# Seven block products for eight in the second product of the second block's MLP

## The chip, the cores and the metric

The kernel runs on one core of a Trainium2 chip. The metric is the device time of one execution in microseconds (us). Names of the engines: PE is TensorE (matrix products), DVE is VectorE, ACT is ScalarE, POOL is GpSimd, SP is the engine that issues most DMAs. SBUF and PSUM are the on-chip memories: products arrive in PSUM, in banks of 128 partitions by 512 fp32 values.

## The reference, cut to what matters

Two transformer blocks follow each other on 512 tokens of width 1024, all in fp32. The change lies in the last stage, the MLP of the second block, whose hidden width is 4096:

```python
def _sq_relu_mlp(h, w1, w2):
    return jnp.square(jax.nn.relu(h @ w1)) @ w2
```

Its result goes through an RMS norm with a gain and is added to the residual stream x, which is the output. `h @ w1` is the first product ("up"), the one with `w2` the second product ("down").

## The kernel before

**Precision.** Every fp32 operand is split into a high and a low part that the one-pass matrix format holds: `split` writes the high part on ACT (L147) and the low part, source less high part, on DVE (L148; for a few weights on POOL). `mm3` (L152 to L154) makes one product out of three matmuls, high by high, high by low, low by high. Weights are split chunk by chunk: a chunk of 128 by 1024 values is fetched by a DMA that SP issues into a raw buffer (two of them), and `parts` takes a buffer for either part out of a ring of PARTS = 5. A chunk can be split only when the one five places ahead of it has been used by PE.

**The MLP** (`mlp`, L822, called at the end of `dense_two`) takes the hidden width in four groups of 1024, that is 8 chunks j of 128. In a group first comes "up": for each j 24 matmuls of 512 columns (8 chunks of the contraction by 3) into a bank `m2up`, then relu on ACT (L843, tile `m2re`), its square on DVE (L844, `m2sq`), and the split of the square (`m2hid`), 512 columns wide. The first five chunks of all run in two token halves, each with 24 matmuls of 256 columns, while the last tokens of h are still being prepared. Then comes "down": hidden activations are the stationary operand, weights `m2d` the moving one. For each of two halves of the output columns, 4 weight chunks by 4 token tiles by 2 by 3 matmuls, 96 in all, each of 512 columns; so 192 to a group. The partial sums (`evac2`) are copied on ACT in group 0 (L1278) and added on DVE to `y` in the other groups (L1280). In the last group every finished half goes on: squares on ACT (L1243), two or three tiny instructions on POOL (L1245 to L1248) for 1 / rms, the gain on DVE (L1288), and x += y / rms on DVE (`post`, L1255), then the output's DMA.

**Around it.** `evac1` closes the output projection ahead of it token tile by token tile: x is fetched, y's squares and 1 / rms (ACT, POOL), x += y / rms (L1255, DVE), x's squares and 1 / rms, then `mod_T` transposes the tile on PE and splits it into `h2T`. x stays in SBUF until the end. The banks of PSUM are dealt out in rings: three for the second product, three for "up".

A scheduler sets the order in which each engine's instructions stand in the program; each engine then works through its own queue in that order.

## Time and profile before

| | us |
|---|---|
| three timed executions | 1271.0, 1275.27, 1275.59 |
| their median | 1275.27 |
| the profiled execution: span from first to last instruction | 1270.8 |

The profile gives no time of its own for the profiled execution beside the span. Its page lists busy time of each engine, the chain of work that ended last, and groups of instructions. A busy PE in it means that matmuls were in flight; how fast they follow each other is read from their starts. The granted clock is the share of full speed that TensorE was granted.

### The profile page before, as it was taken

Reading aid. Unit: us, or ns where it says so; the run is one execution under the profiler, and the core shown is the slowest. Engines: PE = TensorE matmul, PEld = TensorE weight load, DVE = VectorE, ACT = ScalarE, POOL = GpSimd, SP = SyncE. Lnnn points to the kernel's source line nnn. Section 1 sums busy time; section 2 is a strip of 40 time slices with the busy share of each in tenths; the row PEclk is TensorE's granted clock in tenths of the full one; section 3 lists DMA queues with packets and bytes.
Section 4 is the critical chain, followed back from the end, with each engine's and each line's share of the span. In section 5 each row is a group of like instructions: output and inputs, shape, how many; then the busy total and the mean of one; then the engine's idle time right before and its main releaser. Section 6 shows DMA issues by size and latency. Waiting matters only on the chain. (4 is left out here: it accounts for less than half of the span.)

```text
span 1270.8 us, 16908 instructions
## 1 busy us (share of the span) xinstructions
PE 1227.1 (97%) x6388; PEld 1027.8 (81%) x6388; DVE 750.8 (59%) x1320; ACT 539.2 (42%) x1032; POOL 257.5 (20%) x328
## 2 busy tenths in 40 slices
PE   7889999999999999999999999999999999999997
PEld 7889887779888788888888777778888888888886
DVE  4799666597897854336364567564752343433534
ACT  6677555434223324235263556454652331422431
POOL 3877551261020000000023114212400000000001
PEclk9899999999999999999999999999999999999999
DMA  5232121464678733143254122215232322412412
GB/s 163 64 73 68 26 63 67 133 186 148 198 239 257 234 100 116 63 131 122 67 176 129 51 67 74 64 59 178 82 117 83 100 100 67 130 69 67 149 50 84
DMA packets 147290, 140.22 MB, mean 110 GB/s; under 512 B 14025, under 2 KB 115160, under 8 KB 147208
## 3 DMA queue, kind: packets, MB, share of 16 engines
q1 hardware_dynamic: 143384, 131.02, 33.4%
q0 software_dynamic: 3824, 8.12, 2.1%
q8 instruction: 50, 0.82, 0.3%
q14 instruction: 32, 0.26, 0.1%
HBM read 134.85 MB, written 4.26 MB: 109 GB/s over the span
## 5 line engine op out<-in xcount | busy, mean ns | idle before, releaser
L898 DVE SCALAR_TENSOR_TENSOR macc<-mod,silu_c,macc 128x1024 f32<-128x1024 f32 x56 | 76.7, 1379 | 13.8 <-DMA mod<-in_w_mod_dram 13.7
L1245 POOL TENSOR_SCALAR ss<-ss 128x1 f32<-128x1 f32 x4 | 1.8, 442 | 328.5 <-ACT sk L1243 328.5
L1280 DVE TENSOR_TENSOR y<-m2d,y 128x512 f32<-128x512 f32 x24 | 16.6, 691 | 60.4 <-PE m2d L154 60.3
L975 DVE SCALAR_TENSOR_TENSOR xa<-m1d,r,xa 128x512 f32<-128x512 f32 x32 | 23.8, 745 | 37.2 <-PE m1d L154 37.2
L147 ACT ACTIVATE m2hid<-m2sq 128x512 fp32r<-128x512 f32 x32 | 20.2, 631 | 38.9 <-DVE m2sq L844 38.9
L147 ACT ACTIVATE m1hid<-m1sq 128x512 fp32r<-128x512 f32 x32 | 20.0, 629 | 38.1 <-DVE m1sq L844 38.1
L918 POOL DMA_DIRECT2D modrows<-mrow x8 | 3.9, 492 | 147.3 <-DVE mrow L916 92.8
L148 DVE TENSOR_TENSOR m2hid<-m2sq,m2hid 128x512 fp32r<-128x512 f32 x32 | 22.1, 691 | 19.0 <-ACT m2hid L147 18.9
L148 DVE TENSOR_TENSOR npl<-t,nph 128x512 fp32r<-128x512 f32 x32 | 21.7, 681 | 16.4 <-ACT nph L147 16.3
L181 POOL TENSOR_SCALAR w<-w,g_attn 128x384 f32<-128x384 f32 x20 | 26.1, 1314 | 11.2 <-DMA w<-in_w_in_dram 6.6
L148 DVE TENSOR_TENSOR m1hid<-m1sq,m1hid 128x512 fp32r<-128x512 f32 x32 | 21.9, 686 | 9.1 <-ACT m1hid L147 9.1
L194 POOL TENSOR_SCALAR p<-p,d 128x512 f32<-128x512 f32 x8 | 14.0, 1752 | 56.6 <-DVE d L1116 26.3
L683 DVE TENSOR_REDUCE mb<-sb 128x1 f32<-128x128 f32 (+3 forms) x32 | 15.6, 486 | 16.7 <-PE sb L680 16.6
L1115 ACT ACTIVATE p<-s,m 128x512 f32<-128x512 f32 x32 | 22.0, 688 | 6.2 <-DVE m L1113 6.2
L685 ACT ACTIVATE pb<-sb,mb 128x128 f32<-128x128 f32 (+3 forms) x32 | 16.8, 525 | 16.4 <-DVE mb L683 16.1
L843 ACT ACTIVATE m1re<-m1up 128x512 f32<-128x512 f32 x32 | 18.6, 582 | 9.0 <-PE m1up L154 8.7
L1069 POOL TENSOR_TENSOR tb<-G,nam 128x256 f32<-128x256 f32 x24 | 17.7, 765 | 22.6 <-DVE m L1109 12.5
L147 ACT ACTIVATE nph<-t 128x512 fp32r<-128x512 f32 x32 | 19.0, 595 | 7.4 <-PE t L1126 7.2
L844 DVE SCALAR_TENSOR_TENSOR m1sq<-m1up,m1re 128x512 f32<-128x512 f32 x32 | 21.8, 681 | 0.1
L844 DVE SCALAR_TENSOR_TENSOR m2sq<-m2up,m2re 128x512 f32<-128x512 f32 x32 | 21.8, 682 | 0.0
L1126 PE MATMUL t<-ident,p 128*128 128x128 f32 x128 | 18.4, 276 | 1.9 <-DVE npl L148 1.9
L147 ACT ACTIVATE pbh<-tb 128x128 fp32r<-128x128 f32 (+3 forms) x32 | 13.8, 434 | 14.9 <-PE tb L703 14.7
(1856 smaller groups left out, 4521.8 us busy)
## 6 DMA issues: line engine op xcount, KB each, us to landing
mod<-in_w_mod_dram SPq DMA_DIRECT2D x48, 512.0 KB, 4.5
m1u<-in_w_up_dram SPq DMA_DIRECT2D x32, 512.0 KB, 4.5
m1d<-in_w_down_dram SPq DMA_DIRECT2D x32, 512.0 KB, 3.6
m2u<-in_w_mlp_in_dram SPq DMA_DIRECT2D x32, 512.0 KB, 4.2
m2d<-in_w_mlp_out_dram SPq DMA_DIRECT2D x32, 512.0 KB, 3.4
w<-in_w_in_dram SPq DMA_DIRECT2D x16, 512.0 KB, 4.2
w<-in_w_in_dram SPq DMA_DIRECT2D x48, 128.0 KB, 2.6
o1w<-in_w_out_dram SPq DMA_DIRECT2D x8, 512.0 KB, 3.6
```

Of the source, the lines that this page charges most:

```text
L147: self.nc.scalar.activation(out=hi, in_=src, func=AF.Copy)
L148: (eng or self.nc.vector).tensor_tensor(out=lo, in0=src, in1=hi.bitcast(F32), op=ALU.subtract)
L181: eng.tensor_scalar(out=rv[:, i], in0=rv[:, i], scalar1=g, scalar2=None, op0=ALU.mult)
L685: ac(out=pr[:, 0:n], in_=s[:, 0:n], func=AF.Exp, bias=m[:, 0:1], accum_out=den[:, 0:1])
L843: ac(out=r, in_=acc, func=AF.Relu)
L844: nc.vector.scalar_tensor_tensor(out=s, in0=acc, scalar=0.0, in1=r, op0=ALU.max, op1=ALU.mult)
L898: nc.vector.scalar_tensor_tensor(out=accs[s], in0=rw, scalar=sc[:, s, k:k + 1], in1=accs[s], op0=ALU.mult, op1=ALU.add)
L975: nc.vector.scalar_tensor_tensor(out=x[t][:, cols], in0=acc, scalar=r2[:, t:t + 1], in1=x[t][:, cols], op0=ALU.mult, op1=ALU.add)
L1069: nc.gpsimd.tensor_tensor(out=tb[:, h, y], in0=G[:, h, ::-1, o:o + 32][:, :, ::-1], in1=nam[:, y, :].unsqueeze(1).to_broadcast([P, 8, 32]) ...
L1115: ac(out=pr, in_=s, func=AF.Exp, bias=m[:, 2:3], accum_out=den[:, 0:1])
L1126: nc.tensor.transpose(out=tps[:, j * P:(j + 1) * P], in_=pr[:, j * P:(j + 1) * P], identity=self.ident)
L1280: nc.vector.tensor_tensor(out=y[t][:, cols], in0=acc, in1=y[t][:, cols], op=ALU.add)
```

## The change

"Down" of the first three groups is done in Strassen's manner (Winograd's form). The group's 1024 hidden columns, 512 tokens and 1024 output columns are each cut in two: even and odd chunks j, tokens 0 to 255 and 256 to 511, columns 0 to 511 and 512 to 1023. Eight products of quarter blocks would give the group's sum; seven are made instead, out of sums and differences of blocks:

- `operands` forms, for every pair of chunks j, four sums of the pair's squares on DVE (L1301 to L1304 of the changed kernel, 128 by 256 values each), and splits them together (128 by 1024). The even chunk's first half is split alone (256), the odd chunk whole (512).
- `block` fetches quarter blocks of the weights; two of the six needed are fetched a second time, so 12 DMAs of 512 KB to a group instead of 8. `less` subtracts blocks on POOL (L1365), eight instructions of 128 by 1024 to a group.
- `times` makes one product: two chunks of weights, two token tiles, 24 matmuls of 512 columns. The order is 1, 5, 6, 2, 4, 3, 7. Each product has its own accumulator of 256 tokens by 512 columns (`Y`), kept over the groups, filled by ACT in group 0 (L1355) and added to by DVE afterwards (L1357): 14 instructions of 128 by 512 to a group instead of 8.
- `join` combines the seven accumulators on POOL into the four quarters of the output, 14 additions of 128 by 512, while the last group's "up" runs. The last group is done plainly, as before, and added to them.
- SBUF is dealt out anew for this: x is written to DRAM in `evac1` (a DMA that POOL issues) and fetched again for the end, and "down" has five banks of PSUM instead of three.

```diff
@@ Build.run @@
+            self.xspill2 = self.dp.tile([SEQ, D], F32, name="xspill2")
...
@@ dense_two @@
-        self.row(gg[:, 1, :], 5)
-        x = [self.xp.tile([P, D], F32, tag=f"x{t}", name=f"xb{t}") for t in range(NT)]
+            x = [self.ep.tile([P, D], F32, tag=f"x{t}", name=f"xb{t}", bufs=1) for t in range(NT)]
...
+                    nc.gpsimd.dma_start(out=self.xspill2[t * P:(t + 1) * P, :], in_=x[t])
+                    self.mod_T(x[t], g, hT, t, f"n4_{t}", rx)
+            self.out_proj_rows(a["w_out_2"][0], self.mixT, evac1, "o2", KPS2)
+        self.banks(a=(0, 1, 2, 3, 4), s=S2)
+        with ExitStack() as ph:
+            self.ep = ph.enter_context(tc.tile_pool(name="ep3", bufs=2, reuse_waits="tile"))
+            self.mlp_seven(hT, a["w_mlp_in_2"][0], a["w_mlp_out_2"][0], y, gg, "m2")
+
+    def mlp_seven(self, hT, w1, w2, y, gg, name):
+        tt = nc.vector.tensor_tensor
+        pt = nc.gpsimd.tensor_tensor
+        G = 8
+        NG = NJ // G
+        quads = [self.quad(f"{name}hid{i}").rearrange("p a b c -> p (a b c)") for i in range(2)]
+        hid = quads + [ep.tile([P, 3584], F32R, tag=f"hid{i}", name=f"{name}hid{i + 2}", bufs=1) for i in range(2)]
+        more = ep.tile([P, 4, 512], F32, tag="more", name=name + "more", bufs=1)
+        Y = {q: [y[i][:, h * 512:h * 512 + 512] for h in range(2)] for i, q in enumerate((2, 3, 4, 6))}
+        Y[1] = [more[:, 0], more[:, 1]]
+        Y[5] = [more[:, 2], more[:, 3]]
+        Y[7] = [gg[:, 1, h * 512:h * 512 + 512] for h in range(2)]
+        sums = gg[:, 0, :].rearrange("p (o t) -> p o t", o=4)
+        def operands(g, p, st):
+            a11, a21, a12, a22 = st[:, 0, 0:256], st[:, 0, 256:512], st[:, 1, 0:256], st[:, 1, 256:512]
+            tt(out=sums[:, 0], in0=a21, in1=a22, op=ALU.add)
+            tt(out=sums[:, 2], in0=a11, in1=a21, op=ALU.subtract)
+            tt(out=sums[:, 1], in0=sums[:, 0], in1=a11, op=ALU.subtract)
+            tt(out=sums[:, 3], in0=a12, in1=sums[:, 1], op=ALU.subtract)
+            hi, lo = parts_of(p)
+            self.split(hi[:, 3:7], lo[:, 3:7], sums)
+            self.split(hi[:, 1:3].rearrange("p o t -> p (o t)"), lo[:, 1:3].rearrange("p o t -> p (o t)"), st[:, 1])
+        def parts_of(p):
+            return [hid[p][:, x * 1792:(x + 1) * 1792].rearrange("p (o t) -> p o t", o=7) for x in range(2)]
+        def plain(j):
+            return hid[j % G // 2][:, j % 2 * 1024:j % 2 * 1024 + 1024].rearrange("p (x t) -> p x t", x=2)
+        def up(j, st):
+            wh, wl = self.weights(f"{name}u{j}", [(0, self.kview(w1, 0, KC, j * P, P))], KC, P, eng=nc.gpsimd if j < WPJ else None)
+            acc = self.ps("s", f"{name}up{j}")
+            nsp = 2 if j < NSP else 1
+            w = SEQ // nsp
+            for sp in range(nsp):
+                cols = slice(sp * w, (sp + 1) * w)
+                for k in range(KC):
+                    hqd = hT[k // 4]
+                    self.mm3(acc[:, cols], wh[:, k, :], wl[:, k, :], hqd[:, k % 4, 0, cols], hqd[:, k % 4, 1, cols], k == 0, k == KC - 1)
+            s = st[:, j % 2]
+            ac(out=s, in_=acc, func=AF.Relu)
+            nc.vector.scalar_tensor_tensor(out=s, in0=acc, scalar=0.0, in1=s, op0=ALU.max, op1=ALU.mult)
+            if j // G == NG - 1:
+                self.split(plain(j)[:, 0], plain(j)[:, 1], s)
+            elif j % 2 == 0:
+                hi, lo = parts_of(j % G // 2)
+                self.split(hi[:, 0], lo[:, 0], s[:, 0:256])
+        def block(g, q, r, c):
+            t = ep.tile([P, 1024], F32, tag="rb", name=f"{name}d{g}{q}{r}{c}", bufs=6).rearrange("p (a b) -> p a b", a=2)
+            j = g * G + 4 * q
+            src = w2[j * P:(j + 4) * P, c * 512:c * 512 + 512].rearrange("(i r p) e -> r p i e", r=2, p=P)[r]
+            nc.sync.dma_start(out=t, in_=src)
+            return t
+        def times(g, n, o, b):
+            accs = [self.ps("a", f"{name}p{g}{n}{tau}") for tau in range(2)]
+            for q in range(2):
+                wh, wl = self.parts(f"{name}w{g}{n}{q}", b[q], 2, 512)
+                for tau in range(2):
+                    rows = slice(tau * P, (tau + 1) * P)
+                    for i in range(2):
+                        hi, lo = parts_of(2 * q + i)
+                        self.mm3(accs[tau], hi[:, o, rows], lo[:, o, rows], wh[:, i, :], wl[:, i, :], q == i == 0, q == i == 1)
+            for tau in range(2):
+                if g == 0:
+                    ac(out=Y[n][tau], in_=accs[tau], func=AF.Copy)
+                else:
+                    tt(out=Y[n][tau], in0=accs[tau], in1=Y[n][tau], op=ALU.add)
+        def down(g):
+            def blocks(r, c):
+                return [block(g, q, r, c) for q in range(2)]
+            def less(out, b, c):
+                for o, x, z in zip(out, b, c):
+                    pt(out=o, in0=x, in1=z, op=ALU.subtract)
+            b11 = blocks(0, 0)
+            times(g, 1, 0, b11)
+            t1 = blocks(0, 1)
+            less(t1, t1, b11)
+            times(g, 5, 3, t1)
+            t2 = blocks(1, 1)
+            less(t2, t2, t1)
+            times(g, 6, 4, t2)
+            b21 = blocks(1, 0)
+            times(g, 2, 1, b21)
+            less(b21, t2, b21)
+            times(g, 4, 2, b21)
+            b22 = blocks(1, 1)
+            times(g, 3, 6, b22)
+            b12 = blocks(0, 1)
+            less(b22, b22, b12)
+            times(g, 7, 5, b22)
+        def join():
+            for out, p, q, op in ((2, 1, 2, ALU.add), (1, 1, 6, ALU.add), (7, 1, 7, ALU.add), (6, 7, 5, ALU.add), (4, 7, 4, ALU.subtract),
+                                  (5, 1, 5, ALU.add), (3, 5, 3, ALU.add)):
+                for tau in range(2):
+                    pt(out=Y[out][tau], in0=Y[p][tau], in1=Y[q][tau], op=op)
+        s_banks = self.rings["s"]
+        self.rings["s"] = s_banks + list(MORE)
+        for g in range(NG):
+            for j in range(g * G, (g + 1) * G):
+                if j == NSP:
+                    self.rings["s"] = s_banks
+                if j % 2 == 0:
+                    st = ep.tile([P, 2, SEQ], F32, tag="st", name=f"{name}sq{j // 2}", bufs=2)
+                up(j, st)
+                if j % 2 == 1 and g < NG - 1:
+                    operands(g, j % G // 2, st)
+            if g < NG - 1:
+                down(g)
+        join()
+        self.row(gg[:, 1, :], 5)
+        x = []
+        for t in range(NT):
+            x.append(ep.tile([P, 1024], F32, tag="rb", name=f"xc{t}", bufs=6))
+            nc.sync.dma_start(out=x[t], in_=self.xspill2[t * P:(t + 1) * P, :])
+        ss2 = [self.small("ss", f"ss2{t}") for t in range(NT)]
+        for half in range(2):
+            def evac(t, acc):
+                z = Y[((2, 3), (4, 6))[t // 2][half]][t % 2]
+                tt(out=z, in0=acc, in1=z, op=ALU.add)
+                r = self.squares(z, ss2[t], half, f"sk{half}{t}", "st")
+                tt(out=z, in0=z, in1=gg[:, 1, half * 512:half * 512 + 512], op=ALU.mult)
+                    for _, c in self.post(x[t], [Y[(2, 4)[t // 2]][t % 2], z], r):
-        self.mlp(hT, a["w_mlp_in_2"][0], a["w_mlp_out_2"][0], evac2, lambda grp: None, "m2")
+            j = (NG - 1) * G
+            self.token_major(f"{name}d{half}", G,
+                             lambda q: self.weights(f"{name}d{half}{q}", [(0, self.kview(w2, j + 2 * q, 2, half * 512, 512))], 2, 512),
+                             lambda i: plain(j + i), evac, half == 1)
-        self.mlp(hT, a["w_mlp_in_2"][0], a["w_mlp_out_2"][0], evac2, lambda grp: None, "m2")
```

All of PE, before and after: 6051 rows of the program became 5979, 72 less; "down" of a group has 168 matmuls instead of 192 in three of four groups. Three places in the order of the program matter for what follows. In the names, `m2w161l` is the low part of the weights of group 1, product 6, second chunk; `m2p` are the products' banks, `m2more`, `y` and `g_post` hold accumulators, and `g_post` also the four sums.

DVE, "down" of group 1, before:

```order
L148 TENSOR_TENSOR m2d110l<-m2d_9974,m2d110h 128x1024
L844 SCALAR_TENSOR_TENSOR m2sq_9841<-m2up_9815,m2re_9840 128x512
L148 TENSOR_TENSOR m2hid_9704<-m2sq_9841,m2hid_9704 128x512
L1280 TENSOR_TENSOR y_8429<-m2d_0_9852,y_8429 128x512
L1280 TENSOR_TENSOR y_8430<-m2d_1_9859,y_8430 128x512
L1280 TENSOR_TENSOR y_8431<-m2d_2_9866,y_8431 128x512
L148 TENSOR_TENSOR m2d111l<-m2d_10008,m2d111h 128x1024
```

and now:

```order
L148 TENSOR_TENSOR m2w161l<-m2d_9991,m2w161h 128x1024
L1304 TENSOR_TENSOR g_post<-m2sq_9830,g_post 128x256
L1357 TENSOR_TENSOR m2more<-m2p_9911,m2more 128x512
L148 TENSOR_TENSOR m2hid_8885<-m2sq_9830,m2hid_8885 128x512
L1357 TENSOR_TENSOR m2more<-m2p_9912,m2more 128x512
L148 TENSOR_TENSOR m2w120l<-m2d_10031,m2w120h 128x1024
L148 TENSOR_TENSOR m2hid_8885<-g_post,m2hid_8885 128x1024
L148 TENSOR_TENSOR m2w121l<-m2d_10033,m2w121h 128x1024
L148 TENSOR_TENSOR m2w140l<-m2d_10031,m2w140h 128x1024
L1357 TENSOR_TENSOR m2more<-m2p_9953,m2more 128x512
L1357 TENSOR_TENSOR m2more<-m2p_9954,m2more 128x512
L1357 TENSOR_TENSOR y_8426<-m2p_9995,y_8426 128x512
```

The low part of the last pair's sums now stands behind the weights of products 6 and 2 and the emptying of product 1's banks; the emptying of product 5's banks stands behind the weights of product 4.

POOL, group 1, where it had nothing between the last `ssx` row of `evac1` and the `ss` rows of the end:

```order
L1365 TENSOR_TENSOR m2d_9947<-m2d_9947,m2d_9907 128x1024
L1365 TENSOR_TENSOR m2d_9949<-m2d_9949,m2d_9909 128x1024
L1365 TENSOR_TENSOR m2d_9989<-m2d_9989,m2d_9947 128x1024
L1365 TENSOR_TENSOR m2d_9991<-m2d_9991,m2d_9949 128x1024
L1365 TENSOR_TENSOR m2d_10031<-m2d_9989,m2d_10031 128x1024
L1365 TENSOR_TENSOR m2d_10033<-m2d_9991,m2d_10033 128x1024
L1365 TENSOR_TENSOR m2d_10109<-m2d_10109,m2d_10149 128x1024
L1365 TENSOR_TENSOR m2d_10111<-m2d_10111,m2d_10151 128x1024
```

All eight are new; `m2d_10031` and `m2d_10033` become the weights of product 4, which DVE splits as `m2w140l` and `m2w141l`.

PE, "down" of group 1, the end of product 5 (banks `m2p_9953` and `m2p_9954`) among product 6:

```order
L152 MATMUL m2p_9953<-m2w151h,m2hid_8885 128x512
L153 MATMUL m2p_9953<-m2w151l,m2hid_8885 128x512
L152 MATMUL m2p_9954<-m2w151h,m2hid_8885 128x512
L153 MATMUL m2p_9954<-m2w151l,m2hid_8885 128x512
L154 MATMUL m2p_9996<-m2w160h,m2hid_8883 128x512
L152 MATMUL m2p_9995<-m2w161h,m2hid_8884 128x512
L153 MATMUL m2p_9995<-m2w161l,m2hid_8884 128x512
L154 MATMUL m2p_9995<-m2w161h,m2hid_8884 128x512
L152 MATMUL m2p_9995<-m2w161h,m2hid_8885 128x512
L153 MATMUL m2p_9995<-m2w161l,m2hid_8885 128x512
L154 MATMUL m2p_9953<-m2w151h,m2hid_8885 128x512
```

The matmuls that need the last pair's sums (`m2hid_8885`) stand behind 53 matmuls of the group's "down" where they need the high part, and behind 63 where they need the low part (the L154 row), not at their place in the code.

## Rows read from the trace of the kernel before

**Rows 1.** The page: span, and busy time of each engine.

```profile
span 1270.8 us, 16908 instructions
PE 1227.1 (97%) x6388; PEld 1027.8 (81%) x6388; DVE 750.8 (59%) x1320; ACT 539.2 (42%) x1032; POOL 257.5 (20%) x328
```

**Rows 2.** The page: the chain that ended last, by engine and by line.

```profile
PE 28%; DVE 1%; ACT 0%; issue 0%; POOL 0%; DVEq 0%; POOLq 0%; ACTq 0%
PE m2up L153 5%; PE m2up L154 5%; PE m2up L152 5%; PE m2d L152 5%; PE m2d L154 5%; PE m2d L153 5%; DVE xb L1255 1%; DVE h2T L148 0%; ACT sj L1243 0%; ACT n_0v L241 0%; DVE n_1v L243 0%; ACT sx L1243 0%; ACT m2u2h L147 0%; PE n_3t L216 0%; PE n_2t L216 0%
```

**Rows 3.** Busy time in stretches: up, down of groups 0 to 3, tail.

```profile
core 0: us, PE busy (x) PEld busy (x) DVE busy (x) ACT busy (x) POOL busy (x), PEclk, DMA share, GB/s
903.60:951.80 48.20, 48.20 (x325) 45.05 (x326) 29.75 (x43) 24.92 (x48) 4.38 (x9) 0.96 0.27 90
...
1085.40:1129.50 44.10, 44.10 (x191) 35.52 (x190) 22.32 (x26) 17.76 (x25) 0.00 (x0) 1.00 0.42 132
1129.50:1174.20 44.70, 44.70 (x194) 36.25 (x193) 12.63 (x15) 7.58 (x9) 0.00 (x0) 1.00 0.20 59
...
1263.10:1270.80 7.70, 0.00 (x1) 0.00 (x0) 2.80 (x4) 0.72 (x2) 0.81 (x2) 0.66 0.19 71
```

**Rows 4.** PE in order of time: start, us; 24 matmuls lie between these two.

```profile
1090.32 0.39 PE L152 MATMUL m2up<-h2T,m2u17h 128*128 128x512 f32 x1
...
1095.92 0.39 PE L152 MATMUL m2up<-h2T,m2u18h 128*128 128x512 f32 x1
```

**Rows 5.** Groups by shape, DVE: busy us, mean ns, idle before.

```profile
L148 DVE TENSOR_TENSOR m2hid<-m2sq,m2hid 128x512 fp32r<-128x512 f32 x32 | 22.1, 691 | 19.0 <-ACT m2hid L147 18.9
L844 DVE SCALAR_TENSOR_TENSOR m2sq<-m2up,m2re 128x512 f32<-128x512 f32 x32 | 21.8, 682 | 0.0
L1280 DVE TENSOR_TENSOR y<-m2d,y 128x512 f32<-128x512 f32 x24 | 16.6, 691 | 60.4 <-PE m2d L154 60.3
L148 DVE TENSOR_TENSOR m2d100l<-m2d,m2d100h 128x1024 fp32r<-128x1024 f32 x1 | 1.2, 1225 | 1.0 <-ACT m2d100h L147 1.0
...
L148 DVE TENSOR_TENSOR kc<-kc,kc 128x256 fp32r<-128x256 f32 x4 | 1.7, 417 | 0.0
```

**Rows 6.** ACT: groups by shape, and one tile's row (ns min/median/max).

```profile
L147 ACT ACTIVATE m2hid<-m2sq 128x512 fp32r<-128x512 f32 x32 | 20.2, 631 | 38.9 <-DVE m2sq L844 38.9
L843 ACT ACTIVATE m2re<-m2up 128x512 f32<-128x512 f32 x32 | 18.5, 579 | 0.0
L147 ACT ACTIVATE m2d300h<-m2d x1: 1062/1062/1062, 1196.4 to 1196.4; 128x1024 fp32r<-128x1024 f32 x1
```

**Rows 7.** POOL, groups by shape; the last is an issue of a DMA.

```profile
L148 POOL TENSOR_TENSOR m1u3l<-m1u,m1u3h 128x1024 fp32r<-128x1024 f32 x1 | 3.4, 3427 | 0.0
L148 POOL TENSOR_TENSOR m2u0l<-m2u,m2u0h 128x1024 fp32r<-128x1024 f32 x1 | 2.4, 2404 | 0.0
L940 POOL TENSOR_TENSOR xg<-xa,g_mlp 128x512 f32<-128x512 f32 x4 | 6.1, 1526 | 10.4 <-issue 9.7 <-DVE xa L938 0.7
L981 POOL DMA_DIRECT2D xspill<-xa x4 | 2.6, 656 | 69.6 <-DVE xa L975 69.5
```

**Rows 8.** DVE in order of time, where POOL works too: start, us.

```profile
272.27 1.28 DVE L898 SCALAR_TENSOR_TENSOR macc<-mod,silu_c,macc 128x1024 f32<-128x1024 f32 x1
...
274.66 6.32 DVE L898 SCALAR_TENSOR_TENSOR macc<-mod,silu_c,macc 128x1024 f32<-128x1024 f32 x2
...
284.49 0.68 DVE L938 TENSOR_TENSOR xa<-o,xa 128x512 f32<-128x512 f32 x1
```

**Rows 9.** POOL in order of time in the same stretch.

```profile
274.19 2.40 POOL L148 TENSOR_TENSOR m1u1l<-m1u,m1u1h 128x1024 fp32r<-128x1024 f32 x1
276.56 3.33 POOL L148 TENSOR_TENSOR m1u2l<-m1u,m1u2h 128x1024 fp32r<-128x1024 f32 x1
...
282.79 3.43 POOL L148 TENSOR_TENSOR m1u3l<-m1u,m1u3h 128x1024 fp32r<-128x1024 f32 x1
```

**Rows 10.** Busy time in stretches as in rows 3, elsewhere: granted clock, DMA.

```profile
860.00:870.00 10.00, 10.00 (x45) 8.11 (x44) 4.52 (x5) 3.67 (x5) 0.19 (x1) 1.00 0.99 371
...
900.00:905.00 5.00, 2.87 (x14) 2.25 (x13) 4.90 (x10) 2.11 (x3) 1.75 (x3) 0.88 0.60 169
905.00:910.00 5.00, 5.00 (x36) 5.00 (x35) 4.13 (x6) 2.54 (x8) 3.38 (x6) 0.78 0.35 95
```

More of the change, by code (lines that the diff above doesn't have):

```diff
@@ L298, in run @@
                 self.xp = ph.enter_context(tc.tile_pool(name="xp2", bufs=1, reuse_waits="tile"))
-                self.ep = ph.enter_context(tc.tile_pool(name="ep2", bufs=2, reuse_waits="tile"))
                 self.dense_two()
@@ L1251, in post @@
-        def post(t, ys, r):
-            for half in range(2):
-                cols = slice(half * 512, half * 512 + 512)
-                nc.vector.scalar_tensor_tensor(out=x[t][:, cols], in0=ys[half], scalar=r, in1=x[t][:, cols],
-                                               op0=ALU.mult, op1=ALU.add)
-                yield half, cols
-        def evac1(half, t, acc):
-            cols = slice(half * 512, half * 512 + 512)
-            if half == 0:
-                nc.sync.dma_start(out=x[t], in_=self.xspill[t * P:(t + 1) * P, :])
-            r = squares(acc, ssq[t], half, f"sj{half}{t}")
-            nc.vector.tensor_tensor(out=y[t][:, cols], in0=acc, in1=gg[:, 0, cols], op=ALU.mult)
-            if half == 1:
-                ss = self.small("rs", f"ssx{t}")
-                for hf, c in post(t, [y[t][:, 0:512], y[t][:, 512:1024]], r):
-                    rx = squares(x[t][:, c], ss, hf, f"sx{hf}{t}")
-                self.mod_T(x[t], g, hT, t, f"n4_{t}", rx)
@@ L1270, in dense_two, with evac1 @@
[L1270 to L1288 removed]
+        with ExitStack() as ph:
+            self.ep = ph.enter_context(tc.tile_pool(name="ep2", bufs=2, reuse_waits="tile"))
+            x = [self.ep.tile([P, D], F32, tag=f"x{t}", name=f"xb{t}", bufs=1) for t in range(NT)]
+            def evac1(half, t, acc):
+                cols = slice(half * 512, half * 512 + 512)
+                if half == 0:
+                    nc.sync.dma_start(out=x[t], in_=self.xspill[t * P:(t + 1) * P, :])
+                r = self.squares(acc, ssq[t], half, f"sj{half}{t}")
+                nc.vector.tensor_tensor(out=y[t][:, cols], in0=acc, in1=gg[:, 0, cols], op=ALU.mult)
+                if half == 1:
+                    ss = self.small("rs", f"ssx{t}")
+                    for hf, c in self.post(x[t], [y[t][:, 0:512], y[t][:, 512:1024]], r):
+                        rx = self.squares(x[t][:, c], ss, hf, f"sx{hf}{t}")
+                    nc.gpsimd.dma_start(out=self.xspill2[t * P:(t + 1) * P, :], in_=x[t])
+                    self.mod_T(x[t], g, hT, t, f"n4_{t}", rx)
+            self.out_proj_rows(a["w_out_2"][0], self.mixT, evac1, "o2", KPS2)
@@ new lines, in dense_two @@
+        self.banks(a=(0, 1, 2, 3, 4), s=S2)
+        with ExitStack() as ph:
+            self.ep = ph.enter_context(tc.tile_pool(name="ep3", bufs=2, reuse_waits="tile"))
+            self.mlp_seven(hT, a["w_mlp_in_2"][0], a["w_mlp_out_2"][0], y, gg, "m2")
+    def mlp_seven(self, hT, w1, w2, y, gg, name):
+        nc = self.nc
+        ac = nc.scalar.activation
+        tt = nc.vector.tensor_tensor
+        pt = nc.gpsimd.tensor_tensor
+        ep = self.ep
+        G = 8
[107 more added lines that the diff above has]
+        ss2 = [self.small("ss", f"ss2{t}") for t in range(NT)]
+        for half in range(2):
+            def evac(t, acc):
[3 more added lines that the diff above has]
+                tt(out=z, in0=z, in1=gg[:, 1, half * 512:half * 512 + 512], op=ALU.mult)
```

43 lines of the change are left out of this document (15 added, 28 removed).

## Prediction

> **What bounds the kernel now.** I read the page's totals first: PE is busy for 1227.1 of 1270.8 us, DVE for 59% [rows 1]. A share over the whole span doesn't say what a stage waits for, so next the chain that ended last: at its head stand six groups of PE, the three matmul lines of `m2up` and of `m2d`, 5% of the span each, then one DVE line with 1% [rows 2]. This chain is the last stage, the one that is changed. Cut into stretches, PE is busy in all of each from 903.6 to 1263.1 us, while DVE is busy for 22.32 of 44.1 us in "up" of group 2 and 12.63 of 44.7 us in "down", ACT for 17.76 and 7.58, POOL for nothing [rows 3]. The stage is bound by the number of matmuls, and three engines have room. What a matmul costs there: the first of j = 17 starts at 1090.32, the first of j = 18, 24 matmuls later, at 1095.92 [rows 4], so 5.60 / 24 = 0.2333 us each. The row's own 0.39 us is not the price, because matmuls overlap. After the last of them come 7.7 us of tail [rows 3].
>
> **The change part by part.** *Taken away:* 3 groups by 24 matmuls of 512 columns, 72 x 0.2333 = 16.8 us. All of it lies on the path, and the matmuls that stay have the same form. That is the whole gain; everything else can only cost.
>
> *DVE, total.* Added per group: 6 more low parts of weights x 1.225 and 6 more emptied banks x 0.691 [rows 5]. For each of four pairs, where two splits of 0.691 stood, there are four sums of 256 columns, a split of 256, one of 512 and one of 1024: 5 x 0.417 + 0.691 + 1.225 - 1.382 = 2.62 [rows 5]; the row of 256 columns is the nearest, from another stage. So 7.35 + 4.15 + 10.5 = 22.0 on top of 22.32 + 12.63 [rows 3]: 56.9 us. The group now takes PE 360 x 0.2333 = 84.0. In group 0 the 14 bank copies lie on ACT instead. ACT gains 6 x 1.062 for weights and under 4 x 1.1 for the pairs, which makes some 36 of 84 [rows 3, 6].
>
> *POOL, and what it does to DVE.* Eight subtractions of 128 x 1024 per group at 2.40 to 3.43 us [rows 7] are 19 to 27 us on an engine that was empty; the 14 additions of `join` at 1.53 are 21 us in the last "up". POOL has the time. But a DVE instruction that reads two tensors of SBUF takes 1.28 us alone and 6.32 us for two, while two such subtractions run on POOL [rows 8, 9]: 3.16 each, a loss of about 1.9 for each instruction of POOL. A DVE instruction that reads a bank of PSUM is not touched: 0.68 us at 284.49, inside POOL's 3.43 from 282.79 [rows 8, 9]. DVE so needs at most 56.9 + 8 x 1.9 = 72 of 84 us, or 84 if every subtraction cost it POOL's longest 3.43. It is near the bound only at that end.
>
> The Trainium skill (SBUF — State Buffer, section "Who interferes with whom") says that a DVE instruction with two SBUF inputs and a GpSimd instruction that reads SBUF shut each other out for a whole instruction, and that one with at most one SBUF input doesn't contend. By it a subtraction could cost DVE its full 2.4 us rather than 1.9, 76 of 84; the trace shows the stall (6.32 for two) and the exception (0.68).
>
> *Latency where "up" turns into "down".* In steady state totals don't stop PE, late operands do. I count from PE's last matmul of "up" in group 1, along the order of DVE's queue. ACT has a weight ahead (1.06), then relu (0.58): 1.7. DVE: square 0.68, two sums of 0.42, to 3.2; the low part of product 6's second weights can only start when the buffer of product 1's first weights is free, after 12 matmuls (2.8) and ACT's 1.06, and ends at 5.1; the last sum 5.5; bank, split, bank (3 x 0.69) 7.6; product 2's first weights 8.8; then the low part of the last pair's sums, 10.0, and 12 to 13.4 if a subtraction stands in the way. Their high part is done by about 7.7 on ACT. PE asks for the high part after 53 matmuls, 12.4 us, and for the low part after 63, 14.7. Margin: 4.7 and 1.3 to 4.7.
>
> The next narrow place: the five banks. Product 2's second accumulator takes the bank of product 5's first one, and PE asks for it after 84 matmuls, 19.6 us. The two emptying instructions stand on DVE behind the first weights of product 4, whose buffer is free after product 5's last matmul (the 65th, 15.2); ACT 1.06, DVE 1.225, to 17.5; the bank is empty at 18.2. Margin 1.4. The subtraction for these weights starts at 8.8 and has until 15.2, so even 3.43 is in time. Group 0 has the same order, but its DVE is dense before it; there the banks are emptied by ACT, which takes that load off. I take 0.3 us of waiting per group, 1.0 in all; the bounds are 0 (nothing here can gain) and what the rivals below charge.
>
> *DMA.* 20 fetches of 512 KB in 84 us are 125 GB/s, and the trace has 371 GB/s in one stretch [rows 10]; from 903.6 on it is at 132 or below [rows 3]. SP works in order, and the fetches for the next group's weights wait for the previous group's subtractions; the next "up" chunks queue behind them but are wanted only two chunks, 11.2 us, into that "up". Taken as nothing.
>
> *x to DRAM.* Four DMA issues on POOL, 0.656 us each [rows 7], stand in `evac1`'s chain of squares. They run while ACT squares the second half, so I take 0.3 us in sum; bounds 0 and 4 x 0.656 = 2.6. The fetch back lies a whole "up", 44 us, ahead of its use. The tail has the same steps in the same order: nothing.
>
> Sum: -16.8 + 1.0 + 0.3 = -15.5 us. The profiled execution would go from 1270.8 to 1255.3. Its span is 4.5 us below the median of the timed runs, 1275.27, and next to the fastest, 1271.0; no row says where the 4.5 come from, so I carry the difference over: 1275.3 - 15.5 = 1259.8.
>
> **The rivals.** *A part is eaten by late operands.* If two subtractions of 3.43 stand in front of the last pair's low part, and that part behind them, the 4.7 become -2.2; the banks behind it are late by about as much again: some 4 us in groups 1 and 2, and 2 in the dense group 0. That gives 1275.3 - 16.8 + 10 = 1268.5. For it: margins of 1.3 and 1.4 us are thin for a queue this long. Against: even with the measured 1.9 per subtraction everything is in time.
>
> *Slower: PE waits for the banks.* One place: the emptying of product 5's banks behind product 4's weights on DVE. If the pair of subtractions runs in series with DVE's splits on both sides, it comes 2 x 3.43 - 1.4 = 5.5 us late in each of three groups, 16.4 us, the whole gain. Behind each such gap the clock would fall too: after PE was busy for only 2.87 of the 5 us from 900, the granted clock was 0.88 and 0.78 in the two stretches of 5 us, so part of that time at 1.2 instead of 2.4 GHz, 1.7 us lost [rows 10]. Together 1275.3 - 16.8 + 16.4 + 5.1 = 1280. It decides from a wait of 5.6 us per group on. Against it: DVE has 12 us per group to spare, and its instructions on PSUM are not slowed.
>
> *The dense start.* From 903.6 to 951.8 DVE was busy for 29.75 of 48.2 us [rows 3]; the new work of four pairs (10.5) and of product 1's, 5's and part of 6's weights makes it nearly full, and the four first subtractions fall in there. If "down" of group 0 starts 5 to 8 us late for that and nothing else happens, 1265 to 1268. This is in the range; I count it to the first rival.
>
> That the change doesn't do what it says is excluded for the number of matmuls, which the program shows (72 less).
>
> **How the numbers follow.** Forecast, with waits of up to 5 us in sum: 0.72. Part eaten (1264.5 to 1272): 0.16. Slower, 1280: 0.07. A time below the forecast's, if the median falls beside the fast 1271.0 and no wait occurs: 1271.0 - 16.8 = 1254.2, 0.05. The range goes from 1254 to 1267.5 and leaves out the rest of the rivals, some 0.17. A measurement of this kernel can tell about 0.5%, 6.4 us: faster by more needs a time below 1268.9, which the forecast, the fast end and over a third of the eaten case give: 0.83. Within 0.5%: 0.11. Slower: 0.06.
>
> **What would show it right or wrong.** Right: stretches of "up" and "down" with PE busy in all of them, groups 0 to 2 shorter by 5.6 us each, matmuls still 0.233 us apart, DVE at 55 to 72 us per group. The step on latency is wrong if PE has idle time ahead of `m2p` matmuls that DVE ended: by the low part of `m2hid`, or by a bank's emptying. The step on POOL is wrong if the low parts of weights take much over 3.2 us beside a subtraction. The front is wrong if PE's idle time before 904 us grows. The forecast falls if those waits come to over 6 us.

## The result, and the profile after

The changed kernel takes 1257.93 us (median of four runs, 1254.9 to 1260.07), the kernel before beside it 1274.51 (four runs, 1271.0 to 1275.59): a ratio of 0.9881, with a 95% interval of 0.9855 to 0.9908. The prediction had 1259.8, a difference of 15.5 us or 0.9878.

The page of the changed kernel, its first lines and the chain that ended last, which answer to [rows 1, 2]:

```profile
span 1258.3 us, 16992 instructions
...
PE 1213.5 (96%) x6316; PEld 1017.5 (81%) x6316; DVE 844.6 (67%) x1410; ACT 567.3 (45%) x1068; POOL 355.1 (28%) x370
...
PE m2up L153 5%; PE m2up L154 5%; PE m2up L152 5%; PE m2p L152 3%; PE m2p L154 3%; PE m2p L153 3%; PE m2d L152 1%; PE m2d L154 1%; PE m2d L153 1%; DVE h2T L148 0%; DVE xb L1244 0%; ACT n_0v L241 0%; DVE n_1v L243 0%; ACT sx L1232 0%; ACT m2u2h L147 0%
```

DVE worked 94 us more, ACT 28, POOL 98, and PE 13.6 less. Still the chain has only PE at its head: the added work lies beside it. The stage in stretches (up to group 0 from the last `o2wx` matmul of the output projection on, "down" and "up" by turns, the last "down", the tail; columns as in [rows 3]):

```profile
901.50:954.43 52.93, 50.81 (x336) 46.89 (x335) 42.05 (x59) 27.67 (x52) 18.88 (x18) 0.97 0.52 165
954.43:993.24 38.81, 38.81 (x169) 31.63 (x168) 30.26 (x26) 21.10 (x29) 20.62 (x7) 1.00 0.41 128
993.24:1038.04 44.80, 44.80 (x194) 36.06 (x193) 30.84 (x41) 21.05 (x29) 4.27 (x2) 1.00 0.46 133
1038.04:1076.84 38.80, 38.80 (x169) 31.62 (x168) 35.37 (x29) 14.59 (x15) 21.14 (x8) 1.00 0.40 131
1076.84:1121.63 44.79, 44.79 (x193) 36.04 (x192) 31.08 (x44) 20.30 (x27) 2.03 (x1) 1.00 0.44 128
...
1205.23:1249.34 44.11, 44.11 (x193) 35.92 (x191) 19.58 (x26) 10.29 (x20) 5.66 (x10) 1.00 0.15 52
1249.34:1258.30 8.96, 0.39 (x2) 0.00 (x0) 2.80 (x4) 0.72 (x2) 1.30 (x2) 0.81 0.25 97
```

PE is busy in the whole of every "up" and "down". "Up" takes 44.8 us, "down" in sevens 38.8. PE's waits from 850 us on, by what ended them, longest first (us in total, times, longest); these are all:

```profile
PE m2up L153 <- DVE h2T L148: 1.5, 1, 1.5
PE n_1t L216 <- DVE n_1x L232: 1.4, 1, 1.4
PE po L152 <- ACT dhl L147: 0.9, 1, 0.9
PE m2up L152 <- DVE y L1265: 0.6, 1, 0.6
PE po L153 <- DVE dhl L148: 0.2, 1, 0.2
```

No `m2p` stands there: PE never waits where "up" turns into "down", nor inside "down". The two profiled executions, stretch by stretch, in us (the cut is the last matmul of the chunk `o2wx` of the output projection; six others follow it):

| stretch | before | after | difference |
|---|---|---|---|
| start to the last `o2wx` matmul | 899.1 | 901.5 | +2.4 |
| from there to the first matmul of "down", group 0 | 52.7 | 52.9 | +0.2 |
| groups 0 to 2, from "down" to the next "down" | 266.9 | 250.8 | -16.1 |
| last "down" to the start of its last matmul | 44.0 | 44.1 | +0.1 |
| from there to the end | 8.1 | 9.0 | +0.9 |
| span | 1270.8 | 1258.3 | -12.5 |

Of the first row, 2.0 us are no effect of the change: up to the first `o2wx` matmul (869.0 before, 871.0 after) only the fetch of one row of gains was moved, and in the profiled executions told of below the last one starts anywhere from 896.5 to 904.5 us. The other 0.4 is one. From the first to the last `o2wx` matmul it takes 30.1 us before, and 30.4 to 30.6 in the changed kernel and in all ten variants, which have its frame. Two of the four issues of x's DMA stand there (884.50 and 894.13), and the queues of DVE and PE have another order from 886 and 891 on; which of the two costs it was not taken apart. PE's wait `n_1t`, 1.4 us in the list above, was shorter before:

```profile
PE n_1t L216 <- DVE n_1x L232: 1.0, 1, 1.0
```

Lengths of such stretches, most of which repeat to a tenth or better, are compared here rather than spans.

### The profile page after: what moved, and what is told of

Same layout as the page of the kernel before. It is cut to its first block, busy times and chain, and to the rows that moved or that the text cites. A ratio compares the mean times of both kernels' runs of the same rounds, so it can differ in the third digit from the quotient of the medians.

```text
span 1258.3 us, 16992 instructions
## 1 busy us (share of the span) xinstructions
PE 1213.5 (96%) x6316; PEld 1017.5 (81%) x6316; DVE 844.6 (67%) x1410; ACT 567.3 (45%) x1068; POOL 355.1 (28%) x370
## 5 line engine op out<-in xcount | busy, mean ns | idle before, releaser
L1365 POOL TENSOR_TENSOR m2d<-m2d,m2d 128x1024 f32<-128x1024 f32 x24 | 71.2, 2981 | 162.2 <-DVE m2w220l L148 51.5
L898 DVE SCALAR_TENSOR_TENSOR macc<-mod,silu_c,macc 128x1024 f32<-128x1024 f32 x56 | 76.1, 1369 | 15.5 <-DMA mod<-in_w_mod_dram 15.2
L147 ACT ACTIVATE m2hid<-m2sq 128x512 fp32r<-128x512 f32 (+1 forms) x32 | 17.6, 551 | 49.1 <-DVE m2sq L1328 49.1
L148 DVE TENSOR_TENSOR m2hid<-m2sq,m2hid 128x512 fp32r<-128x512 f32 (+1 forms) x32 | 24.3, 760 | 6.0 <-ACT m2hid L147 5.8
L1069 POOL TENSOR_TENSOR tb<-G,nam 128x256 f32<-128x256 f32 x24 | 17.8, 774 | 22.1 <-DVE m L1109 12.5
L685 ACT ACTIVATE pb<-sb,mb 128x128 f32<-128x128 f32 (+3 forms) x32 | 16.8, 525 | 16.0 <-DVE mb L683 15.7
L152 PE MATMUL pj<-w_0h,xnT 128*128 128x384 f32 (+1 forms) x48 | 18.0, 376 | 4.9 <-ACT pjs L407 3.9
L981 POOL DMA_DIRECT2D xspill<-xa x4 | 2.6, 655 | 70.0 <-DVE xa L975 69.9
L1328 DVE SCALAR_TENSOR_TENSOR m2sq<-m2up,m2sq 128x512 f32<-128x512 f32 x32 | 21.9, 684 | 0.0
```

Source lines behind the costliest of these rows:

```text
L147: self.nc.scalar.activation(out=hi, in_=src, func=AF.Copy)
L148: (eng or self.nc.vector).tensor_tensor(out=lo, in0=src, in1=hi.bitcast(F32), op=ALU.subtract)
L152: mm(out=out, lhsT=lh, rhs=rh, start=start, stop=False)
L898: nc.vector.scalar_tensor_tensor(out=accs[s], in0=rw, scalar=sc[:, s, k:k + 1], in1=accs[s], op0=ALU.mult, op1=ALU.add)
L1328: nc.vector.scalar_tensor_tensor(out=s, in0=acc, scalar=0.0, in1=s, op0=ALU.max, op1=ALU.mult)
L1365: pt(out=o, in0=x, in1=z, op=ALU.subtract)
```

## The experiments

The theory: PE is bound by the number of its matmuls, the 72 that are gone are the whole gain, and all that was added is covered. Its rivals: the new frame (banks, x by way of DRAM) gives or costs something of its own; POOL's subtractions cost time, in front of the weights or through DVE; margins at the turns are so thin that a part is lost. All variants start from the changed kernel, and the runs of the kernel before stand beside each.

**No group in sevens (sevens_0).**

```diff
+        NS = 0
-                if j % 2 == 1 and g < NG - 1:
+                if j % 2 == 1 and g < NS:
...
+            if g < NS:
                 down(g)
...
+                def gather(t, acc):
+                    z = Y[((2, 3), (4, 6))[t // 2][half]][t % 2]
...
+                self.token_major(f"{name}d{g}{half}", G,
...
```

A group from NS on is made as the last one is, and `gather` copies or adds its banks into the four quarters.

> No group is done in sevens: the second product is made of eight plain products in all four groups, in the frame of the changed kernel (x written to DRAM and fetched again, five banks, the same tail). It tells the count of matmuls from everything else that came with the change. Theory (PE is bound by its matmuls, the 72 that are gone are the whole gain): groups of 88.8 us as in the kernel before, time within 2 us of it, 1272 to 1277. Rival (the new frame, five banks above all, gives part of the gain): well below the kernel before, 1262 to 1270. Rival (the frame costs): 1278 or more.

Measured 1274.88 us, 1.0014 of the kernel before (0.9995 to 1.0033). The groups take 88.93, 88.95 and 88.96 us, against 88.81, 88.89 and 89.22 before. Group 0's "down", and the "up" behind it:

```profile
953.57:997.71 44.14, 44.14 (x194) 36.11 (x192) 11.10 (x10) 13.64 (x17) 0.00 (x0) 1.00 0.31 93
997.71:1042.50 44.79, 44.79 (x193) 36.04 (x192) 18.86 (x22) 16.83 (x24) 0.00 (x0) 1.00 0.30 97
```

The frame alone gives nothing, and costs at most a few us. From here to the changed kernel only the sevens differ, with the sums, subtractions, fetches, emptied banks and joins that belong to them, and the three groups go from 266.84 to 250.80 us.

**Without the subtractions (no_sub).**

```diff
             def less(out, b, c):
-                for o, x, z in zip(out, b, c):
-                    pt(out=o, in0=x, in1=z, op=ALU.subtract)
+                return
```

> The subtractions of weight blocks on POOL are left out, so that the products are made with the blocks as fetched; nothing else changes. Theory (they are covered, on POOL and in what they do to DVE): time as the changed kernel within 1.5 us, groups of 83.6 us, DVE's busy time per group falls from about 66 to about 57 us. Rival (subtractions in front of weights, or DVE held up by them, cost PE time): faster than the changed kernel by more than 2 us.

Measured 1257.03 us, 0.9877 (0.9845 to 0.9909). Groups 0 to 2, without the subtractions and, behind them, of the changed kernel:

```profile
955.76:1039.37 83.61, 83.61 (x362) 67.64 (x360) 47.29 (x59) 42.31 (x57) 0.00 (x0) 1.00 0.43 125
1039.37:1122.97 83.60, 83.60 (x362) 67.64 (x361) 54.88 (x72) 35.12 (x43) 0.00 (x0) 1.00 0.43 127
1122.97:1206.57 83.60, 83.60 (x362) 67.64 (x361) 52.72 (x56) 33.13 (x40) 24.49 (x15) 1.00 0.38 120
...
954.43:1038.04 83.61, 83.61 (x362) 67.69 (x361) 61.10 (x66) 42.15 (x58) 24.90 (x8) 1.00 0.44 131
1038.04:1121.63 83.59, 83.59 (x361) 67.67 (x360) 66.45 (x72) 34.89 (x42) 23.17 (x8) 1.00 0.42 129
1121.63:1205.23 83.60, 83.60 (x361) 67.68 (x360) 60.85 (x56) 32.65 (x40) 35.99 (x19) 1.00 0.39 121
```

The lengths are the same. Beside POOL's own time only DVE's (the third of those with a count) falls much, in group 1 by 66.45 - 54.88 = 11.6 us, 1.45 for each subtraction; in groups 0 and 2 it is 13.8 and 8.1. They cost DVE time, and the kernel none.

**The subtractions on DVE (sub_dve).** In `less`, `tt` stands for `pt`.

> The eight subtractions of a group stand on DVE instead of POOL. Theory: DVE's own work rises by 8 x 1.23 to about 67 us of 84 per group, but it is no longer held up by POOL, so its busy time stays near 66; time as the changed kernel within 2 us. Rival (DVE's queue has no margin at the turn from up to down): PE idles ahead of the m2p matmuls, each group is 2 us or more longer, 1264 or more.

Measured 1258.7 us, 0.9878 (0.9848 to 0.9909). Groups 1 and 2 take 83.60 us each, with DVE at 63.61 us in group 1: eight of its own instructions (1.22 us each) cost it a little less than POOL's did. Group 0 takes 85.77, since one wait appears there, 1.6 us: `m2p` on the high part of the last pair's sums, which ACT forms from what DVE hands over. It is the first narrow place of the prediction, in the dense group that it named. It costs something only here, where two subtractions stand ahead of the last pair's fourth sum in DVE's own queue (at 962.85 and 967.27, the sum at 968.41 to 968.83). About half of the wait has another source: ACT's queue now has the copy of a bank, which waits for PE until 969.12, ahead of the split, and the split starts at 969.61.

**Three banks (three_banks).**

```diff
-        self.banks(a=(0, 1, 2, 3, 4), s=S2)
+        self.banks(a=(0, 1, 2), s=S2)
```

> The second product has three banks, as in the kernel before, instead of five. It asks how much of the margin in front of PE is the banks'. With three, the second accumulator of a product takes the bank of the product before, which DVE must have emptied some 12 matmuls (2.8 us) after its last one. Theory of the prediction (emptying may stand behind a chunk of weights on DVE, and then has no margin): PE idles 1 to 3 us at several of the seven products, groups of 86 to 95 us, 1265 to 1290. Rival (DVE empties banks at once, so that banks are no limit at all): as the changed kernel within 2 us.

Measured 1259.53 us, 0.9893 (0.9861 to 0.9925). PE waits for a bank twice in group 0 (1.0 us ahead of product 5, 0.2 ahead of product 6, for ACT) and once in each of the others (0.3 ahead of product 6, for DVE); groups of 85.3, 84.1 and 84.1 us. The theory's 86 to 95 was too much in every group, and the rival's time came: a bank is mostly empty in time. By the groups five banks are worth 2.7 us; the times, 1.6 us apart, can't tell that from nothing.

**Every subtraction twice (sub_twice).**

```diff
                     pt(out=o, in0=x, in1=z, op=ALU.subtract)
+                    pt(out=o, in0=o, in1=z, op=ALU.subtract)
```

> Every subtraction of weight blocks is made twice on POOL, the second time on its own result, so that the products are of other blocks; it doubles POOL's work and what that costs DVE. A single subtraction costs DVE 1.45 us in the changed kernel ((66.45 - 54.88) / 8, group 1 with and without them). Theory (what is off PE is covered as long as operands are in time): DVE at 54.9 + 16 x 1.45 = 78 of 83.6 us, POOL at 45 to 50; PE idles 0 to 1 us per group, 1257 to 1262. Rival (margins of 1.5 us in front of the banks and the weights of product 4 decide): PE idles 3 to 6 us per group ahead of m2p matmuls, 1267 to 1277.

Measured 1282.38 us, 1.0082 of the kernel before (1.006 to 1.0103): the whole gain and more is lost. Groups of 89.46, 87.88 and 91.72 us instead of 83.6. From the last `o2wx` matmul to the first "down" it takes 57.9 us, against 51.3 in the two runs that have the same granted clock at the start of it, those without sevens and without subtractions: 6.6 us. PE's waits in groups 1 and 2:

```profile
PE m2p L152 <- ACT m2w270h L147: 3.3, 1, 3.3
PE m2p L153 <- DVE m2w170l L148: 1.6, 1, 1.6
PE m2p L153 <- DVE m2w270l L148: 1.6, 1, 1.6
PE m2p L152 <- ACT m2w170h L147: 0.7, 1, 0.7
```

In these two groups all are for the first weights of product 7 (`m2w170`, `m2w270`), not for product 4's or a bank. Why, POOL in order of time shows (group 1; its "down" begins at 1049.28):

```profile
1066.36 3.74 POOL L1366 TENSOR_TENSOR m2d<-m2d 128x1024 f32<-128x1024 f32 x2
1074.12 5.67 POOL L1365 TENSOR_TENSOR m2d<-m2d,m2d 128x1024 f32<-128x1024 f32 x2 [4.03 <-DVE m2w130l L148]
1079.75 4.73 POOL L1366 TENSOR_TENSOR m2d<-m2d,m2d 128x1024 f32<-128x1024 f32 x2
```

POOL is idle for 4 us, until DVE has made `m2w130l`, the low part of product 3's first weights. The difference for product 7 is written over block b22, which product 3 still reads. Then come subtractions, ACT and DVE in series, with PE waiting at the end. Group 0 is not so plain: there PE waits for the last pair's sums (1.1 us), for product 4's weights (0.9) and for product 7's (2.4). In the dense start it waits 3.4 us for an "up" weight that ACT has behind the split of a pair's sums. These sums are late: POOL subtracts without a pause from 926 to 948 us, and on DVE even a sum of 256 columns, 0.42 us alone, then takes up to 2.62:

```profile
943.18 5.38 POOL L1366 TENSOR_TENSOR m2d<-m2d,m2d 128x1024 f32<-128x1024 f32 x2
943.69 2.62 DVE L1303 TENSOR_TENSOR g_post<-g_post,m2sq 128x256 f32<-128x256 f32 x1
```

The theory's expectation was wrong. The rival's waits came about as long as it said, 2.3 to 4.9 us per group, but its time was 5 us too short, with the dense start left out of it, and its place was right only in part of group 0.

**The same, with the difference written elsewhere (sub_twice_apart).**

```diff
-            less(b22, b22, b12)
-            times(g, 7, 5, b22)
+            less(b12, b22, b12)
+            times(g, 7, 5, b12)
```

> As the run with every subtraction made twice (1282.4 us, PE idle 2.3 and 4.9 us ahead of product 7 in groups 1 and 2), with one thing changed: the difference for product 7 is written over block b12 instead of b22. Product 3 also reads b22, so writing there has to wait until both its chunks are split (POOL starts 0.1 us after that split, at 1074.12 in that run), writing to b12 doesn't. The products are again of other blocks. Theory (the narrow place is this wait behind product 3's splits, not the amount of work on POOL or DVE): POOL starts some 3 to 4 us sooner, the idle time ahead of product 7 goes in group 1 and most of it in group 2, 1266 to 1275; what is lost in group 0 stays. Rival (POOL at 45 us per group and DVE at 78 are too much in themselves): 1279 to 1285.

Measured 1271.08 us, 1.0001 (0.9982 to 1.002). POOL comes to that subtraction 19.5 us after the start of "down" instead of 24.8, and groups 1 and 2 take 85.1 and 84.4 us, with 0.5 us of waiting for product 7 left. In groups 1 and 2 the amount of work on POOL and DVE was bearable, as the theory had it; the wait behind product 3's splits was the narrow place. Group 0 stays at 89.6. PE waits there for the last pair's sums (1.3 us) and for weights of products 4, 3 and 7 (0.9, 0.8 and 0.3), and once more in the "up" behind them (0.8). The dense start is as dear as in the run before this one, with 3.7 us of waiting for the same "up" weight.

**The gain into a separate buffer (tail_z).**

```diff
-                tt(out=z, in0=z, in1=gg[:, 1, half * 512:half * 512 + 512], op=ALU.mult)
+                s = z
+                if half == 1:
+                    z = Y[(1, 5)[t // 2]][t % 2]
+                tt(out=z, in0=s, in1=gg[:, 1, half * 512:half * 512 + 512], op=ALU.mult)
```

> The second half of a token tile takes its gain into a separate buffer, as in the kernel before, instead of in place, so that DVE's multiplication needn't wait until ACT's square has read it; nothing else changes. Theory (the multiplication in place is what makes the tail longer): from the start of the last matmul to the end 7.9 to 8.1 us instead of 9.0, time 0.6 to 1 us below the changed kernel, which rounds can hardly tell. Rival (the tail is longer for another reason, the five banks or the order of the finishing steps): 9.0 us as before.

Measured 1255.82 us, 0.988 (0.9859 to 0.9901); runs can't tell that from the changed kernel. The trace can: the tail takes 8.5 us, between the theory's 8.1 at most and the rival's 9.0. After the last matmul, the changed kernel and then this one (start, us, what, and what ended the wait before it):

```profile
1249.76 0.69 DVE L1414 TENSOR_TENSOR y<-m2d,y 128x512 f32<-128x512 f32 x1 [1.10 <-PE m2d L154]
...
1251.30 0.69 DVE L1416 TENSOR_TENSOR y<-y,g_post 128x512 f32<-128x512 f32 x1 [0.85 <-ACT sk L1232]
1251.37 0.75 POOL L1236 TENSOR_SCALAR ss<-ss 128x1 f32<-128x1 f32 x1 [4.16 <-ACT sk L1232]
...
1253.57 0.99 SPq L1419 DMA_DIRECT2D out_dram<-xc  x2
```

```profile
1246.99 0.69 DVE L1414 TENSOR_TENSOR y<-m2d,y 128x512 f32<-128x512 f32 x1 [1.59 <-PE m2d L154]
1247.72 0.69 DVE L1419 TENSOR_TENSOR m2more<-y,g_post 128x512 f32<-128x512 f32 x1
...
1248.60 0.27 POOL L1236 TENSOR_SCALAR ss<-ss 128x1 f32<-128x1 f32 x1 [4.65 <-ACT sk L1232]
...
1250.31 0.99 SPq L1422 DMA_DIRECT2D out_dram<-xc  x2
```

From the last addition to the last issue it is 3.81 and 3.32 us; before the change it was also 3.32. In place, DVE's multiplication must wait for ACT's square, and then runs at the same time as POOL's tiny instruction, which takes 0.75 us instead of 0.27. That is 0.5 of the 0.9 us of tail. The other 0.4 lie behind the last issue, 4.7 us to the end against 4.3, here as there; what makes them stays open.

**The last group in sevens too (three versions).** With `join` where it is, after the last product (sevens_4_join_last):

> All four groups in sevens, with the join on POOL as it stands, after the last product, and then all token tiles closed. Theory: 5.5 us of matmuls less, but ten of the 14 additions on POOL wait for the last product (1.3 to 2.3 us each, some 16 us) and the closing of eight halves follows (some 12 us instead of 8); 1268 to 1278, so the gain is lost behind the last matmul. Rival (DVE and ACT close tiles while POOL still joins, so that only a few us are added): 1258 to 1264.

One execution, 1270.74 us. PE is through sooner, 38.6 us after the group's first `m2p` matmul, and then 26.0 us of tail follow: the gain goes behind the last matmul, as the theory had it.

With the joins spread over the last products (sevens_4). `close` makes a product (its number, its operand, its weights) and adds its banks to quarters that POOL has joined already; for each it gets the quarter, the first token tile and the half, and closes it:

```diff
+        close(7, 5, b12, ((4, 2, 0), (6, 2, 1)))
+        close(2, 1, b21, ((2, 0, 0),))
+        close(3, 6, b22, ((3, 0, 1),))
```

> The last group is done in sevens as well. Its products run in the order 1, 5, 6, 4, 7, 2, 3, the accumulators are joined on POOL as soon as their products are there, the banks of products 7, 2 and 3 are added straight to what is joined, and token tiles 2 and 3 are closed while products 2 and 3 run. Theory (PE is bound by its matmuls): 24 fewer by 0.23 us, 5.5 us less; the last two token tiles end 2.8 us apart instead of 5.5, which may cost 1 to 2 us of tail; 1253 to 1255, the last matmul 5.3 us after its group's first m2p matmul sooner than now. Rival (joins of the last group come too late, the tail grows by what is saved): 1257 to 1262.

Measured 1264.72 us, 0.9948 (0.9929 to 0.9967), 7 us worse than the changed kernel and above both expectations. The last matmul comes 45.9 us after the first `m2p`, and 14.7 us of tail follow. DVE's and PE's longest waits in the last group:

```profile
DVE y L1444 <- POOL y L1429: 4.9, 1, 4.9
...
PE m2p L152 <- DVE y L1444: 4.3, 1, 4.3
```

POOL's joins are late, DVE's additions wait for them, and PE waits for a bank.

With `join` of the first three groups left in the last "up", and the last banks added straight to the quarters (sevens_4_joined_before; `adds` names the quarters, and those that are closed then):

```diff
+                if j == (NG - 1) * G:
+                    join()
...
+        last(6, 4, t2, adds((3, 4, 6)))
+        last(4, 2, t2, adds((4,), m))
+        last(7, 5, b12, adds((4, 6), p, {4: (2, 0), 6: (2, 1)}))
+        last(2, 1, b21, adds((2,), p, {2: (0, 0)}))
+        last(3, 6, b22, adds((3,), p, {3: (0, 1)}))
```

> All four groups in sevens, but the join of the first three groups stays where it is in the changed kernel, on POOL during the last up. The last group's products are then added straight to the four quarters: DVE adds banks to 1, 2 or 3 quarters, only products 1 and 1 + 5 are kept and added by POOL, early (8 additions). The difference for product 7 is written over b12, in a buffer of the squares, whose fetch waits for nothing. Order 1, 5, 6, 4, 7, 2, 3; the gain goes to a separate buffer as in the run with the separate buffer. Theory (the first version with four groups lost because DVE, and behind it PE, waited 4.9 us for POOL's join, and because the closing steps then piled up): PE has no wait in the last group, 24 matmuls by 0.23 us are gone from that run's 1255.8, the tail is 0 to 2 us longer; 1250 to 1252.5. Rival (DVE can't close four halves of tiles 2 and 3 beside the last products' weights): 1255 or more.

Measured 1261.45 us, 0.9905 (0.9878 to 0.9933): the rival's time, and not told apart from the changed kernel. PE waits for the last pair's sums (1.6 us) and for a bank (1.5), its last matmul comes after 43.3 us, hardly sooner than the plain group's 44.1, and the tail takes 12.5 us, since DVE has a dozen closing steps queued when PE ends. One row of several shows how the sums come late, a difference of 256 columns on DVE that takes 2.41 us beside the weight subtraction that POOL has at 1207.86, where such a one takes 0.42 alone:

```profile
1208.14 2.41 DVE L1303 TENSOR_TENSOR g_post<-m2sq 128x256 f32<-128x256 f32 x1
```

The last group has no next "up" behind which its sums and closings could lie. None of the versions tried here makes it cheaper than doing it plainly.

## Why the prediction held, point by point

**The gain, -16.8.** The mechanism is shown: with the frame held and only the sevens added, the three groups lose 266.84 - 250.80 = 16.0 us. The size was off by 0.8, and the step is the price of a matmul. It was read in "up" [rows 4], 0.2333 us; the matmuls taken away are "down's". In the run without sevens "down" takes 44.14 us for 192 of them (953.57 to 997.71), 0.2299 each, so 72 are 16.55. The other 0.5 is that those that stay now take 38.81 / 168 = 0.2310.

**Late operands, +1.0.** Measured 0, the lowest bound that was given. The working behind it held closely. The low part of the last pair's sums was forecast 10.0 us after PE's last "up" matmul; in group 1 it ends at 1047.81, 9.8 us after "down" begins at 1038.04. The banks of product 5 were to be empty at 18.2; they are at 1055.96, 17.9. Such margins were then treated as if something would eat them, and nothing does. The first rival (a part eaten, 1268.5) did not occur.

**DVE and POOL.** DVE was put at 56.9 us per group without POOL's effect and 72 at most with it; measured in group 1, 54.9 and 66.5. Low parts of weights take up to 3.42 us beside a subtraction, a little over the 3.2 that was named as a sign. POOL's subtractions take 2.98 us on average, within the 2.40 to 3.43 given [rows 7]:

```profile
L1365 POOL TENSOR_TENSOR m2d<-m2d,m2d 128x1024 f32<-128x1024 f32 x24 | 71.2, 2981 | 162.2 <-DVE m2w220l L148 51.5
```

How the two hinder each other can be read in group 1, POOL and then DVE in order of time:

```profile
1059.51 2.41 POOL L1365 TENSOR_TENSOR m2d<-m2d,m2d 128x1024 f32<-128x1024 f32 x1 [5.83 <-DVE m2w130l L148]
1063.08 2.40 POOL L1365 TENSOR_TENSOR m2d<-m2d,m2d 128x1024 f32<-128x1024 f32 x1 [1.16 <-DVE m2w131l L148]
1065.65 3.19 POOL L1365 TENSOR_TENSOR m2d<-m2d,m2d 128x1024 f32<-128x1024 f32 x1 [0.16 <-POOL m2d L1365]
```

```profile
1060.12 2.88 DVE L148 TENSOR_TENSOR m2w131l<-m2d,m2w131h 128x1024 fp32r<-128x1024 f32 x1
1062.93 0.68 DVE L1357 TENSOR_TENSOR y<-m2p,y 128x512 f32<-128x512 f32 x1
1063.53 3.04 DVE L148 TENSOR_TENSOR m2w170l<-m2d,m2w170h 128x1024 fp32r<-128x1024 f32 x1
1066.49 0.68 DVE L1357 TENSOR_TENSOR y<-m2p,y 128x512 f32<-128x512 f32 x1
1067.09 2.83 DVE L148 TENSOR_TENSOR m2w171l<-m2d,m2w171h 128x1024 fp32r<-128x1024 f32 x1
```

Each split ends 1.1 us after the subtraction that it meets: POOL ends at 1061.92, 1065.48 and 1068.84, DVE at 1063.00, 1066.57 and 1069.92, whatever DVE's start was. So in these rows DVE waits until POOL's instruction is over and then needs nearly what it needs alone (1.22). POOL's third, 3.19 instead of 2.40, waits in the same way for DVE's end at 1066.57. The addition out of a bank, at 1066.49, keeps its 0.68. This is what the Trainium skill (SBUF — State Buffer, "Who interferes with whom") says; the 2.4 per subtraction that followed from it is the price of a full meeting. The 1.45 measured is less because each of the eight splits that a subtraction held up in group 1 began at another point of it: they lost 0.3 to 2.2 us.

**DMA, 0.** It held: no wait of PE in the list above ends in a DMA.

**x to DRAM, +0.3, and the dense start.** Measured 0.6: 0.4 while the output projection still runs, and 0.2 from its last `o2wx` matmul to the first "down" (52.9 us after 52.7), which the dense start shares.

**The tail, 0.** Wrong by 0.9 us: "the same steps in the same order" overlooked that `z` is now multiplied in place. That makes 0.5, as the run with the separate buffer shows.

**The slower rival, 1280.** It did not occur, but its mechanism exists. Doubled subtractions bring it about, with PE idle for 2.3 and 4.9 us in groups 1 and 2 and the clock behind it at 0.66 and 0.54 of full speed (5 us from 1085 and from 1175 of that run), as [rows 10] had it in kind. The place was the weights of product 7, not the banks behind product 4's weights: the working asked when the buffers for weights come free, and not whether a block can be written over while another product reads it. In the changed kernel itself product 7 has room: its first low part ends at 1066.57 and is used at 1071.5.

**The sum.** -16.1 for the three groups and +1.6 for front, last "down" and tail make -14.5 in the trace, against -15.5. It came so near in part by luck: pitch, front, last "down" and tail were put 2.0 too low together, and the 1.0 for waits that didn't come made up for half of that. The medians differ by 16.6, with an interval (11.7 to 18.5) wide enough for both. Of the 4.5 us that were carried over from span to median, a part stands between the span and the time of any one execution: in each later profiled execution the time on record is 1.7 to 2.8 us above its span.

## What to carry to other kernels

Where one engine is busy in all of a stage, count what is taken from it, at the pitch of the very stretch it is taken from; the cover for what is added is then a matter of each operand's place in its queue, not of totals. A difference formed in place inherits a wait for every reader of the buffer; writing it over the other operand took 11 us off a loaded version of this kernel. An arithmetic saving with sums behind it belongs in the groups that have another stage after them; in the last one, in the three versions tried here, sums and closing steps took the gain.
